# Four plain columns moved ahead of the pairs in down, a 256-column entry for each up quarter, another order of joining, and the ple gate's pairs amid its plain rows

## The chip, the cores and the metric

The kernel runs on one core of a Trainium2 chip. The metric is the device time of one execution in microseconds (us). The kernel before took 1455.88 us, the median of 3 runs (1454.91 to 1456.17). TensorE multiplies matrices, VectorE (DVE in rows, "Vector" here) and ScalarE (ACT) work on tiles, GpSimd (POOL) starts some transfers and SyncE (SP) most of them.

## What is computed

One layer of a decoder trunk on 256 tokens and 2048 channels. The part that the change touches is the channel mixer and the per-layer embedding gate:

```python
u = rmsnorm(h, g_ffn_pre[i])
up = causal_depthwise_conv(u @ w_up[i], conv_w[i], conv_b[i])
gate_ff, value = jnp.split(up, [D_FF], axis=-1)
f = (jax.nn.gelu(gate_ff, approximate=True) * value) @ w_down[i]
h = h + rmsnorm(f, g_ffn_post[i])
e = p[i] @ w_ple_in[i]
h = h + jax.nn.sigmoid((h @ w_ple_gate[i]).astype(jnp.float32)).astype(h.dtype) * e
```

Ahead of it stand two kinds of attention, their gates and an output projection, which are left as they were. D_FF is 5632, so up has 88 columns of 128 channels (gate and value in turn) and down has 44 rows of 128 by 16 columns of 128.

## The kernel before, in words

All numbers are float32. To multiply with enough digits, each operand is split into a high half, which TensorE reads as fp32r, and a low half, the rest. A product is then three matmuls: high by high, low by high, high by low. `three_wide` (L925) does this with 512 columns each. In up (`mul`, L359 on), the activations' two halves lie side by side, 512 columns, so that one 128x128 weight block costs one matmul of 512 columns with the weight's high half (L364) and one of 256 with its low half (L366).

Weights come as tiles of 128x1024, eight blocks, packed in the order of `_plan`. For each tile SP loads `raw` (`load`, L194; 5 buffers), ScalarE writes the high half (`high`, L228) and Vector the low half (`low`, L283; 7 buffers for each half). Whenever TensorE's instruction list comes to a new tile, `tick` runs: it queues deferred work (evacuations of finished banks), the high half of the tile six further on, and the low halves five further on. So the list of each engine interleaves weight preparation with the rest, and the sixth tile ahead can be written only when TensorE has left the tile whose buffer it takes.

The mixer goes in four quarters. In a quarter, up makes 22 columns of 16 blocks each. Each column is summed, scaled, convolved and passed through gelu by ScalarE and Vector in three or four ticks (`up_evac`), which ends in a row of `ft`; there are 11 rows. Then down multiplies the 11 rows by 16 columns:

- the first 8 columns by `strassen` (L1236): rows 0 to 7 make four pairs. A pair takes 21 matmuls of 512 columns where plain ones would be 24, needs sums of weights (two extra tiles a pair, added by Vector at L244 to L248 or by accumulating transfers of POOL into `tsum`, L263), and sums of activations (`mixed`), and collects into seven of the eight banks of 2 KB: P1, P5, P6, P7 and three that go straight to results. After the pairs the rows 8 to 10 follow as plain products ("plains", 36 matmuls) into four result banks. The products are put together by Vector: `join` in quarter 0 (4 operations, L1285 to L1288) or `join_to` later (8, L1294 to L1301), and then `ends` (4, L1305).
- the columns 8 to 11 and 12 to 15 by `four` (L1307), 66 matmuls each into two banks. Their evacuation is two operations, on ScalarE in quarter 0 and on Vector after that (L1394).

In the last quarter the squares of the finished columns (L1344) and their weighing by the gain (`weigh`, L1348) are deferred between these steps; the last two banks are added at L1417, the norm is worked out, applied (L1411) and transposed by TensorE (L1437), while TensorE multiplies the e columns (`e_cols`).

The ple gate (`pg`) does columns 0 to 3 plainly, columns 4 to 11 with `strassen` over 16 rows: rows 8 to 15 plainly, then rows 0 to 7 as four pairs, `join` and `ends` at once, and columns 12 to 15 with `four`. `finish` (L1502 to L1504) multiplies by e, adds h and sends out.

One more detail: where the 512- and 256-column matmuls of up begin after other work, `mm` can do the first eight blocks as three matmuls of 256 columns each (`even=8`, `mul1`, L384 to L386) and turn one later block round (`turned=9`, L363). This pair of settings is called `SETTLE` (L38), and before the change only the column in quarter 0 at which the norm's scale becomes known uses it.

Of the kernel before, what the change touches and what calls it, by code (L numbers as in the profile page):

```python
# [8 lines left out]
F32 = mybir.dt.float32  # L9
F32R = mybir.dt.float32r  # L10
AF = mybir.ActivationFunctionType
OP = mybir.AluOpType
# [35 lines left out]
def _plan():  # L48
# [47 lines left out]
    for q in range(NQ):  # L96
        for n in range(max(FIRST, q * 2 * QT), (q + 1) * 2 * QT):
            add(("up", n), [up[n]], KT)
        rows = list(range(q * QT, (q + 1) * QT))
        down = [("w_down", j) for j in range(KT)]  # L100
        plan.append((("pairs", "down", q), down[:8],
                     paired([(rows[r], rows[r + 1]) for r in range(0, DROWS, 2)]) + whole(rows[DROWS:])))
        for c in (8, 12):
            add(("down", q, c), down[c:c + 4], 0, [[r] for r in rows])
    for c in range(2, 4):
# [4 lines left out]
                 whole(range(2 * PAIRS, KT)) + paired([(2 * p, 2 * p + 1) for p in range(PAIRS)])))  # L110
# [24 lines left out]
def hybrid_block_kernel(ctx: ExitStack, tc: tile.TileContext, head, gx, pT, convp, bias, masks, gains, w, out):  # L135
# [20 lines left out]
    stream, used, sums_of, early_sums = [], 0, {}, []  # L156
    for g in _plan():
        if _pairs(g):
            assert used % 8 == 0
            before = KT - 2 * PAIRS if g[0][:2] == ("pairs", "pg") else 0  # L160
# [16 lines left out]
    half_raw = {sums_of[i] for i in by_dma}  # L177
    place = {r: i for i, r in enumerate(stream) if r is not None}

# [1056 lines left out]
    def strassen(key, src, pairs, plain, first_plain, p1_to):  # L1236
# [11 lines left out]
        def plains(last):  # L1248
            for k in plain:
                w2 = item()  # L1250
                for t in range(2):
                    for n in range(2):
                        add((t, n), cut(src, k, t), w2[n], last and k == plain[-1])

        if first_plain:
            plains(False)
        for p, (k1, k2) in enumerate(pairs):
# [6 lines left out]
            add((0, 1), s[3], w22, last and first_plain)  # L1264
# [7 lines left out]
            add((0, 0), cut(src, k2, 0), w21, last and first_plain)  # L1272
        yield bk
        if not first_plain:
            plains(True)
# [14 lines left out]
    def join_to(o, bk, x):  # L1290

        tt = DVE.tensor_tensor
        x2 = tmp.tile([128, 512], F32, name="x2", tag="s2", bufs=2)
        tt(o[0, 0], o[0, 0], x, OP.add)  # L1294
        tt(x, bk[6], x, OP.add)
        tt(x2, bk[7], x, OP.add)  # L1296
        tt(o[1, 0], o[1, 0], x2, OP.add)
        tt(x, bk[5], x, OP.subtract)
        tt(x2, bk[5], x2, OP.subtract)
        tt(o[0, 1], o[0, 1], x, OP.add)  # L1300
        tt(o[1, 1], o[1, 1], x2, OP.add)  # L1301

    def ends(o, bk):
        for at in ((0, 0), (0, 1), (1, 0), (1, 1)):
            DVE.tensor_tensor(o[at], o[at], bk[at], OP.add)  # L1305

# [47 lines left out]
    for q in range(NQ):  # L1354
        for n in range(max(len(pss), q * 2 * QT), (q + 1) * 2 * QT):
            ps = mm(keys[n], u2, **dict(SETTLE, mid={3: mid}) if n == len(pss) else {})
# [5 lines left out]
        o = quarter(0)  # L1362
        x = o[0, 0] if q == 0 else tmp.tile([128, 512], F32, name="x1", tag="s2", bufs=2)
        s = strassen(("pairs", "down", q), ft, [(r, r + 1) for r in range(0, DROWS, 2)], range(DROWS, QT), False, x)
        bk = next(s)
        defer((None, (lambda bk=bk, o=o: join(o, bk)) if q == 0 else lambda bk=bk, o=o, x=x: join_to(o, bk, x)))
        if end:
            g3 = []
            for n, name in enumerate(("wsum", "tsum")):
                g3.append(fp.tile([128, 1024], F32, name="g3", tag=name))  # L1370
                nc.sync.dma_start(g3[n], gains[:, n * 1024:(n + 1) * 1024])
        next(s)
        defer((None, lambda bk=bk, o=o: ends(o, bk)))
        if end:
            ACT.preload_act_table_set(LNEXP)
            squared(range(2))
        for c in (2, 3):
# [5 lines left out]
            four(("down", q, 4 * c), ps, ft, hold if end and c == 3 else None)  # L1383
            if end and c == 3:
                break
# [9 lines left out]
            defer((lambda evac=evac: evac(False), lambda evac=evac: evac(True)))  # L1395
            if end:
                squared([c])
# [97 lines left out]
    for n in range(PAIRS):  # L1495
        mixture(n)

# [12 lines left out]
    defer((lambda ps=ps: sigmoid(ps, 0), lambda: finish([(t, 0, 512) for t in range(2)])))  # L1510
    o = quarter(512)
    s = strassen(("pairs", "pg"), u3, [(2 * p, 2 * p + 1) for p in range(PAIRS)], range(2 * PAIRS, KT), True, o[0, 0])
    bk = next(s)
    join(o, bk)
    ends(o, bk)
    next(s, None)
# [84 lines left out]
```

## Time and profile before

| | |
|---|---|
| median of 3 runs | 1455.88 us |
| the profiled execution | 1454.63 us |
| its span, first to last instruction | 1452.5 us |
| up, quarter 0, from its settled column on | 642.25 to 731.36 us |
| down, quarters 0 to 3, start | 731.36, 920.37, 1103.82, 1287.64 us |
| down, quarters 0 to 3, end | 796.01, 979.46, 1163.28, 1346.27 us |
| ple gate's last pair's last product to its last matmul | 1418.52 to 1447.53 us |
| mean granted TensorE clock | 0.999 of full speed |

A window's row gives the stretch, its length, the busy time of an engine with its number of instructions, the clock granted to TensorE, the share of the transfer engines' time and GB/s. A row of the timeline gives the start, the length, the engine, the line, the operation with output and input, and in brackets the idle time before it and what ended it. A row of waits gives who waited for whom: the total, how often, the longest.

### The profile page before, as it was taken

To read this page: it belongs to the slowest core of one execution; us is meant where nothing else is said; L and a number is where in the kernel's file an instruction comes from. 1 tells how busy PE (TensorE), PEld (TensorE's weight loads), DVE (VectorE), ACT (ScalarE), POOL (GpSimd) and SP (SyncE) were. 2 spreads that over 40 slices of the span, in tenths; PEclk is the share of its full clock that TensorE was granted. 3 is DMA by queue.
4 is the path that set the end of the run, shared out by engine and by line. 5 is a ranking of instruction groups with operands and counts; after the bars stand their busy time and mean duration, and the time that the engine had idled before them with its cause. 6 is when DMAs were issued, how large, how long until landed. Compare 5 with 4: busy or idle time off the path is not lost.

```text
span 1452.5 us, 20479 instructions
## 1 busy us (share of the span) xinstructions
PE 1433.1 (99%) x7475; PEld 1221.6 (84%) x7475; DVE 1166.5 (80%) x1785; ACT 860.3 (59%) x1295; POOL 39.4 (3%) x49
## 2 busy tenths in 40 slices
PE   9999999999999999999989999999999999999997
PEld 8888888888888888998867888878888788888786
DVE  7876666669889865879996888977889778899696
ACT  7665555566556655676665566645566456566653
POOL 0000000011010000000000000000000000000000
PEclk9999999999999999999999999999999999999999
DMA  7755746479895766464658565586554855558562
GB/s 290 261 176 164 239 151 213 154 235 263 281 248 179 265 238 194 151 237 162 196 176 281 181 190 173 159 284 188 188 180 147 284 187 189 182 138 298 167 219 113
DMA packets 87188, 298.60 MB, mean 206 GB/s; under 512 B 9648, under 2 KB 10288, under 8 KB 86960
## 3 DMA queue, kind: packets, MB, share of 16 engines
q1 hardware_dynamic: 80752, 285.76, 58.4%
q0 software_dynamic: 6336, 11.54, 4.7%
q8 instruction: 59, 0.97, 0.3%
q14 instruction: 41, 0.34, 0.1%
HBM read 294.11 MB, written 3.15 MB: 205 GB/s over the span
## 4 chain that ended last, share of the span: by engine, by line
PE 92%; DVE 3%; DMA 2%; ACT 1%; issue 1%; ACTq 0%; DVEq 0%
PE mm L364 33%; PE mm L927 25%; PE mm L366 17%; PE mm L692 2%; PE mm L690 2%; PE mm L691 2%; PE mm L845 2%; PE mm L847 2%; PE mm L846 2%; DMA raw<-in_w 2%; DVE lo L283 1%; ACT hi L228 1%; DVE lo L275 1%; PE S L364 0%; PE S L703 0%
## 5 line engine op out<-in xcount | busy, mean ns | idle before, releaser
L283 DVE TENSOR_TENSOR lo<-raw,hi 128x1024 fp32r<-128x1024 f32 (+1 forms) x497 | 581.9, 1187 | 115.3 <-ACT hi L228 110.7
L364 PE MATMUL mm<-u,hi 128*128 128x512 f32 x1828 | 643.2, 396 | 0.0
L228 ACT ACTIVATE hi<-raw 128x1024 fp32r<-128x1024 f32 (+1 forms) x497 | 504.5, 1028 | 192.1 <-PE mm L364 61.7
L366 PE MATMUL mm<-u,lo 128*128 128x256 f32 x1818 | 509.9, 281 | 0.0
L364 PEld LDWEIGHTS mm<-u,hi 128*128 128x128 f32 x1828 | 342.3, 188 | 80.1
L366 PEld LDWEIGHTS mm<-u,lo 128*128 128x128 f32 x1818 | 343.4, 189 | 0.8 <-DVE lo L283 0.2
L927 PE MATMUL mm<-hi,ft 128*128 128x512 f32 x544 | 172.4, 391 | 4.1 <-DVE x L1296 2.8
L927 PE MATMUL mm<-hi,u 128*128 128x512 f32 x456 | 147.6, 394 | 3.8 <-DVE ff L1285 3.8
L422 ACT ACTIVATE t<-mm 128x256 f32<-128x256 f32 x131 | 49.8, 380 | 154.3 <-PE mm L366 154.3
L927 PEld LDWEIGHTS mm<-hi,ft 128*128 128x128 f32 x544 | 102.1, 188 | 27.3 <-DVE x L1296 4.0
L927 PE MATMUL mm<-lo,ft 128*128 128x512 f32 x272 | 106.8, 393 | 2.6 <-DVE lo L283 2.6
L927 PEld LDWEIGHTS mm<-hi,u 128*128 128x128 f32 x456 | 86.4, 190 | 22.1 <-DVE ff L1285 4.3
L425 DVE TENSOR_TENSOR s<-mm,t 128x256 f32<-128x256 f32 x116 | 48.9, 422 | 59.7 <-ACT t L422 59.5
L927 PE MATMUL mm<-lo,u 128*128 128x512 f32 x228 | 89.5, 393 | 0.0
L364 PE MATMUL mm<-mg,hi 128*128 128x512 f32 x232 | 80.5, 392 | 0.0
L224 ACT ACTIVATE hi<-wsum 128x512 fp32r<-128x512 f32 x84 | 51.1, 630 | 49.2 <-DVE wsum L247 38.9
L366 PE MATMUL mm<-mg,lo 128*128 128x256 f32 x230 | 64.4, 280 | 0.0
L927 PEld LDWEIGHTS mm<-lo,ft 128*128 128x128 f32 x272 | 51.0, 188 | 15.1 <-DVE lo L283 4.8
L1205 ACT ACTIVATE cv<-cpad,cw 128x256 f32<-128x256 f32 x88 | 52.5, 597 | 10.9 <-DVE cpad L1200 10.7
L275 DVE TENSOR_TENSOR lo<-wsum,hi 128x512 fp32r<-128x512 f32 x84 | 54.3, 685 | 0.3
L927 PE MATMUL mm<-hi,mixed 128*128 128x512 f32 x160 | 52.8, 391 | 0.0
L364 PEld LDWEIGHTS mm<-mg,hi 128*128 128x128 f32 x232 | 43.3, 187 | 9.3
(327 smaller groups left out, 1799.6 us busy)
## 6 DMA issues: line engine op xcount, KB each, us to landing
raw<-in_w SPq DMA_DIRECT2D x479, 512.0 KB, 4.0
gh<-in_w SPq DMA_DIRECT2D x12, 512.0 KB, 5.0
gh<-in_w POOLq DMA_DIRECT2D x24, 256.0 KB, 8.2
raw<-in_w SPq DMA_DIRECT2D x22, 256.0 KB, 3.6
tsum<-in_w SPq DMA_DIRECT2D x10, 512.0 KB, 3.5
tsum<-in_w POOLq DMA_DIRECT2D x20, 256.0 KB, 6.7
hd<-in_head SPq DMA_DIRECT2D x6, 576.0 KB, 7.5
gh<-in_gx SPq DMA_DIRECT2D x6, 512.0 KB, 4.7
```

The source lines that it names most:

```text
L224: ACT.activation(hi[i][:, n * 512:(n + 1) * 512], x, AF.Copy)
L228: ACT.activation(hi[i][:, a:b], raw[i][:, a:b] if src is None else src, AF.Copy)
L275: DVE.tensor_tensor(lo[i][:, to], x, f(hi[i][:, to]), OP.subtract)
L283: DVE.tensor_tensor(lo[i][:, a:b], raw[i][:, a:b] if src is None else src, f(hi[i][:, a:b]), OP.subtract)
L364: PE.matmul(ps, wh, rhs, start=first, stop=last, skip_group_check=True)
L366: PE.matmul(ps[:, :T], wl, rhs[:, :T], start=False, stop=last, skip_group_check=True)
L422: ACT.activation(t1[0], ps[:, T:], AF.Copy)
L425: DVE.tensor_tensor(out, ps[:, :T], t1[0], OP.add)
L690: PE.matmul(pv[t], xh, wh, start=kt == 0, stop=False)
L691: PE.matmul(pv[t], xh, wl, start=False, stop=False)
L927: PE.matmul(ps, x[i], w[j], start=first and n == 0, stop=last and n == 2, skip_group_check=True)
L1205: ACT.activation(y, c[:, 2:], AF.Identity, scale=cw[:, n, 2:3], bias=cw[:, n, 3:4])
```

## The change

Down, in each quarter: columns 8 to 11 are multiplied first, then the pairs, the plains, and columns 12 to 15. Since 44 blocks are five and a half tiles, each of the two groups of four columns is followed by a pad of four blocks that no one reads; the tile with it is loaded and split at half width (`short`). In the last quarter the squares and weighings move accordingly: those of columns 8 to 11 behind the pairs, those of columns 0 to 7 into columns 12 to 15.

Up: the first column of every quarter uses `SETTLE`.

Joining: `join_to` reads the bank of P6 first, then P7, then P5, and the pairs' products of a tile (P6 and a result) change places.

Ple gate: `strassen` takes rows 8 to 13 ahead of the pairs and rows 14 and 15 behind them; `join`, `ends` and the first columns' `finish` are deferred; the sums of activations are deferred behind the first columns' sigmoid.

```diff
+        add(("down", q, 8), down[8:12], 0, [[r] for r in rows])
+        add("pad", down[:4], 0, [rows[:1]])
         plan.append((("pairs", "down", q), down[:8],
                      paired([(rows[r], rows[r + 1]) for r in range(0, DROWS, 2)]) + whole(rows[DROWS:])))
-        for c in (8, 12):
-            add(("down", q, c), down[c:c + 4], 0, [[r] for r in rows])
+        add(("down", q, 12), down[12:], 0, [[r] for r in rows])
+        add("pad", down[:4], 0, [rows[:1]])
...
-                 whole(range(2 * PAIRS, KT)) + paired([(2 * p, 2 * p + 1) for p in range(PAIRS)])))
+                 whole(range(8, 14)) + paired([(2 * p, 2 * p + 1) for p in range(PAIRS)]) + whole(range(14, KT))))
...
-    half_raw = {sums_of[i] for i in by_dma}
     place = {r: i for i, r in enumerate(stream) if r is not None}
+    short = {place[r] for r in short}
+    half_raw = {sums_of[i] for i in by_dma} | short
+    part |= short
...
-    def strassen(key, src, pairs, plain, first_plain, p1_to):
+    def strassen(key, src, pairs, before, after, p1_to):
...
             t2, t4 = item()
+            add((1, 0), cut(src, k2, 1), t4)
             add(6, s[1], t2, last)
-            add((1, 0), cut(src, k2, 1), t4, last and first_plain)
...
+        tt(x2, bk[6], x, OP.add)
         tt(o[0, 0], o[0, 0], x, OP.add)
-        tt(x, bk[6], x, OP.add)
-        tt(x2, bk[7], x, OP.add)
-        tt(o[1, 0], o[1, 0], x2, OP.add)
+        tt(x, bk[7], x2, OP.add)
+        tt(x2, bk[5], x2, OP.subtract)
+        tt(o[1, 0], o[1, 0], x, OP.add)
         tt(x, bk[5], x, OP.subtract)
-        tt(x2, bk[5], x2, OP.subtract)
-        tt(o[0, 1], o[0, 1], x, OP.add)
-        tt(o[1, 1], o[1, 1], x2, OP.add)
+        tt(o[0, 1], o[0, 1], x2, OP.add)
+        tt(o[1, 1], o[1, 1], x, OP.add)
...
-            ps = mm(keys[n], u2, **dict(SETTLE, mid={3: mid}) if n == len(pss) else {})
+            settle = n in (len(pss), q * 2 * QT)
+            ps = mm(keys[n], u2, **SETTLE if settle else {}, mid={3: mid} if n == len(pss) else None)
...
+        plain(2)
         o = quarter(0)
...
+            ACT.preload_act_table_set(LNEXP)
+            squared([2])
         next(s)
         defer((None, lambda bk=bk, o=o: ends(o, bk)))
         if end:
-            ACT.preload_act_table_set(LNEXP)
             squared(range(2))
-        for c in (2, 3):
...
+        ps = plain(3)
...
-    defer((lambda ps=ps: sigmoid(ps, 0), lambda: finish([(t, 0, 512) for t in range(2)])))
+    defer((lambda ps=ps: sigmoid(ps, 0), None))
+    for n in range(PAIRS):
+        mixture(n)
...
     bk = next(s)
-    join(o, bk)
-    ends(o, bk)
-    next(s, None)
+    defer((None, lambda bk=bk, o=o: join(o, bk)))
+    next(s)
+    defer((None, lambda bk=bk, o=o: ends(o, bk)))
+    defer((None, lambda: finish([(t, 0, 512) for t in range(2)])))
```

The order in which the instructions now stand, at three places. The lines of the changed kernel are 6 to 15 higher (L364, L366, L283, L927 are L370, L372, L289, L933). The first place is TensorE in quarter 0, where up ends and down begins. `mm` are banks, `u2` up's activations, `hi` and `lo` weight tiles' halves, `ft` the rows, `mixed` the pairs' sums. Before:

```order
L366 MATMUL mm_7138<-u2_4823,lo_6994 128x256
L927 MATMUL mm_7209<-hi_7023,ft_5995 128x512
L927 MATMUL mm_7209<-lo_7024,ft_5995 128x512
L927 MATMUL mm_7209<-hi_7023,ft_5995 128x512
L927 MATMUL mm_7213<-hi_7023,mixed_6177 128x512
L927 MATMUL mm_7213<-lo_7024,mixed_6177 128x512
```

Now, at the place where the pairs begin, 66 matmuls further on:

```order
L933 MATMUL mm_7188<-lo_7163,ft_5995 128x512
L933 MATMUL mm_7188<-hi_7162,ft_5995 128x512
L933 MATMUL mm_7322<-hi_7191,ft_5995 128x512
L933 MATMUL mm_7322<-lo_7192,ft_5995 128x512
L933 MATMUL mm_7322<-hi_7191,ft_5995 128x512
L933 MATMUL mm_7326<-hi_7191,mixed_6177 128x512
```

The pairs' first tile (`hi_7023` before, `hi_7191` now) stood directly behind up's last block; now it stands behind the four columns' last row.

The second place is TensorE where quarter 1 of up begins, now; `u` are up's activations.

```order
L933 MATMUL mm<-hi,ft 128x512
L390 MATMUL mm<-u_4823,hi 128x256
L391 MATMUL mm<-u_4823,hi 128x256
L392 MATMUL mm<-u_4823,lo 128x256
```

Before, the first block of that column was L364 and L366, 512 and 256 columns, straight after down's last matmul; now eight blocks of three 256-column matmuls come first, then the turned one.

The third place is Vector at the end of down in the last quarter: `lo` and `u3` are low halves of tiles, `ff` the result, `g3` the gain, `sm` small sums of the norm. Before:

```order
L283 TENSOR_TENSOR u3_12431<-raw_12771,u3_12431 128x1024
L283 TENSOR_TENSOR lo_12818<-raw_12789,hi_12817 128x1024
L1394 TENSOR_TENSOR ff_5994<-ff_5994,mm_12713 128x512
L1394 TENSOR_TENSOR ff_5994<-ff_5994,mm_12714 128x512
L283 TENSOR_TENSOR lo_12850<-raw_12809,hi_12849 128x1024
L1348 TENSOR_TENSOR ff_5994<-ff_5994,g3_12646 128x512 x2
L283 TENSOR_TENSOR lo_12874<-raw_12823,hi_12873 128x1024
L1413 TENSOR_REDUCE sm_6178<-sm_6178 128x2
```

Now:

```order
L289 TENSOR_TENSOR u3_12464<-raw_12801,u3_12464 128x1024
L1309 TENSOR_TENSOR ff_5994<-ff_5994,mm_12646 128x512
L1309 TENSOR_TENSOR ff_5994<-ff_5994,mm_12605 128x512
L1309 TENSOR_TENSOR ff_5994<-ff_5994,mm_12630 128x512
L1309 TENSOR_TENSOR ff_5994<-ff_5994,mm_12821 128x512
L289 TENSOR_TENSOR lo_12872<-raw_12833,hi_12871 128x1024
L1357 TENSOR_TENSOR ff_5994<-ff_5994,g3_12792 128x512 x4
L289 TENSOR_TENSOR lo_12908<-raw_12855,hi_12907 128x1024
L289 TENSOR_TENSOR lo_12930<-raw_12877,hi_12929 128x1024
L1427 TENSOR_REDUCE sm_6178<-sm_6178 128x2
```

The evacuation of columns 8 to 11 (L1394) is gone from the end, and the `ends` (L1309, formerly L1305) and the weighing of columns 0 to 7 (four operations, L1357) stand there, which used to lie one group of four columns earlier. Between the join's eighth operation and L1427 there are now a low half, two weighings, a low half, one of half width, and the rows shown.

More of the change, by code (lines that the diff above doesn't have):

```diff
@@ L1246, in add, with plains @@
             three_wide(bk[name], x, w, first, last)
-        def plains(last):
-            for k in plain:
+        def plains(ks):
+            for k in ks:
                 w2 = item()
@@ L1252, in plains @@
                     for n in range(2):
-                        add((t, n), cut(src, k, t), w2[n], last and k == plain[-1])
-        if first_plain:
-            plains(False)
+                        add((t, n), cut(src, k, t), w2[n], k == after[-1])
+        plains(before)
         for p, (k1, k2) in enumerate(pairs):
@@ L1263, in strassen @@
                 ACT.activation(p1_to, bk[1], AF.Copy)
-            add((0, 1), s[3], w22, last and first_plain)
+            add((0, 1), s[3], w22)
             q, t3 = item()
@@ L1268, in strassen @@
             t2, t4 = item()
+            add((1, 0), cut(src, k2, 1), t4)
             add(6, s[1], t2, last)
-            add((1, 0), cut(src, k2, 1), t4, last and first_plain)
             w21, _ = item()
-            add((0, 0), cut(src, k2, 0), w21, last and first_plain)
+            add((0, 0), cut(src, k2, 0), w21)
         yield bk
-        if not first_plain:
-            plains(True)
+        plains(after)
         yield bk
@@ L1305, in ends, with pad @@
             DVE.tensor_tensor(o[at], o[at], bk[at], OP.add)
+    def pad():
+        assert next(plan)[0] == "pad"
+        at["block"] += 4
     def four(key, ps, src, late=None):
@@ L1361, in hybrid_block_kernel, with plain @@
             lend(1, u3)
[L1362 to L1374, printed above, removed]
-            ACT.preload_act_table_set(LNEXP)
-            squared(range(2))
-        for c in (2, 3):
+        def plain(c):
             ps = [bank() for _ in range(2)]
@@ L1382, in hold @@
                 at["hold"] = True
-            four(("down", q, 4 * c), ps, ft, hold if end and c == 3 else None)
-            if end and c == 3:
-                break
+            last = end and c == 3
+            four(("down", q, 4 * c), ps, ft, hold if last else None)
+            pad()
+            if last:
+                return ps
             def evac(low, ps=ps, q=q, c=c):
@@ L1394, in evac @@
                             DVE.tensor_tensor(to, to, ps[t], OP.add)
-            defer((lambda evac=evac: evac(False), lambda evac=evac: evac(True)))
-            if end:
-                squared([c])
+            defer((lambda: evac(False), lambda: evac(True)))
+        plain(2)
+        o = quarter(0)
+        x = o[0, 0] if q == 0 else tmp.tile([128, 512], F32, name="x1", tag="s2", bufs=2)
+        s = strassen(("pairs", "down", q), ft, [(r, r + 1) for r in range(0, DROWS, 2)], [], range(DROWS, QT), x)
+        bk = next(s)
+        defer((None, (lambda bk=bk, o=o: join(o, bk)) if q == 0 else lambda bk=bk, o=o, x=x: join_to(o, bk, x)))
+        if end:
+            g3 = []
+            for n, name in enumerate(("wsum", "tsum")):
+                g3.append(fp.tile([128, 1024], F32, name="g3", tag=name))
+                nc.sync.dma_start(g3[n], gains[:, n * 1024:(n + 1) * 1024])
+            ACT.preload_act_table_set(LNEXP)
+            squared([2])
+        next(s)
+        defer((None, lambda bk=bk, o=o: ends(o, bk)))
+        if end:
+            squared(range(2))
+        ps = plain(3)
     flush()
```

13 lines of the change are left out of this document (8 added, 5 removed).

## The prediction

> **What bounds the kernel now.** I read the page first: its busy times and the chain of work that ended last.
>
> ```profile
> PE 1433.1 (99%) x7475; PEld 1221.6 (84%) x7475; DVE 1166.5 (80%) x1785; ACT 860.3 (59%) x1295; POOL 39.4 (3%) x49
> ...
> PE 92%; DVE 3%; DMA 2%; ACT 1%; issue 1%; ACTq 0%; DVEq 0%
> ```
>
> TensorE carries 92% of the chain, so a change gains only where TensorE stands still or its matmuls follow each other more slowly than they could. The 99% hides that, since a matmul counts as busy for 0.39 us while the next one starts much earlier: the chain, in order of time, has 91 matmuls of 512 columns in 20.63 us, 0.2267 us from start to start. With that price I asked for the windows of the stages that the change touches: down of the four quarters (252 matmuls each, counted with the neighbours at the edges), then the tail of the ple gate (102 of its matmuls).
>
> ```profile
> 1329.89 20.63 PE mm L927 x91
> ```
>
> ```profile
> 731.36:796.01 64.65, 59.74 (x254) 1.00 0.74 233
> 920.37:979.46 59.09, 57.95 (x254) 1.00 0.70 236
> 1103.82:1163.28 59.46, 58.01 (x255) 1.00 0.69 234
> 1287.64:1346.27 58.63, 57.93 (x254) 1.00 0.69 237
> 1418.52:1447.53 29.01, 25.18 (x103) 0.94 0.28 109
> ```
>
> 252 x 0.2267 is 57.1 us. The four downs lose 7.5, 2.0, 2.3 and 1.5 us, 13.3 together; the gate's tail, 23.1 us of work, loses 5.7 (its last matmul runs 0.2 past its successor's place). The waits of TensorE name Vector in all of them:
>
> ```profile
> PE mm L927 <- DVE ff L1285: 3.8, 1, 3.8
> PE mm L927 <- DVE x L1296: 2.8, 3, 1.3
> PE mm L927 <- DVE lo L283: 2.6, 3, 1.4
> PE mm L927 <- DVE ff L1286: 1.3, 1, 1.3
> ```
>
> L283 writes the low halves of weight tiles, which the pairs of quarter 0 wait for; L1285, L1286 and L1296 read a product's bank in the join, and the next four plain columns want that bank. The last view is the up columns:
>
> ```profile
> 642.25:731.36 89.11, 89.11 (x525) 1.00 0.56 183
> 796.01:920.37 124.36, 124.36 (x705) 1.00 0.57 180
> ...
> 1163.28:1287.64 124.36, 124.36 (x706) 1.00 0.58 180
> ```
>
> Quarter 0's last 16 columns take 89.11 us, 5.55 each without the 0.24 of two foreign matmuls; quarters 1 to 3 take 124.36 for 22, 5.65 each, with no wait at all. The same 16 blocks of a 512- and a 256-column matmul come at 0.3467 us each in the one train and 0.3533 in the other. The fast train is the one that began with 256-column matmuls.
>
> **The entry to up.** Its rows in quarter 0:
>
> ```profile
> 642.25 0.28 PE L384 MATMUL mm<-u,hi 128*128 128x256 f32 x1
> ...
> 643.32 0.40 PE L520 MATMUL mm<-sp,ones 128*128 128x256 f32 x2
> 643.56 0.28 PE L384 MATMUL mm<-u,hi 128*128 128x256 f32 x1
> ...
> 645.36 0.40 PE L364 MATMUL mm<-u,hi 128*128 128x512 f32 x1
> ...
> 646.42 0.40 PE L364 MATMUL mm<-u,hi 128*128 128x512 f32 x1
> ```
>
> Eight entry blocks take 3.11 less 0.24, 2.87 us; the three up to the turned one 1.06; the other 341 blocks of a quarter, at 0.3467, 118.2. That is 122.1 against 124.36: 2.2 us a quarter, **6.6 us for three**. If the slow train went on regardless, the entry would cost 0.05 a quarter. I take the fast train, since the trace's only example of this entry led to it. The Trainium skill ("TensorE: Matmul & The Clock Gate", Back-to-back issue gap) lets the spacing depend on the columns alone, N/2.4 + 2.5 ns; by it the entry does nothing, and the sum below would be 6.6 us smaller. The trace does not agree as it stands: equal blocks differ by 6.6 ns.
>
> **Four plain columns ahead of the pairs.** A pair is 21 matmuls, 4.8 us, and eats four tiles of high and low halves, so in the pairs Vector can only live on the lead that it has. In quarter 0 it has little: the sum of the last up column starts 6.9 us after the column's end at 731.36, in quarter 1 only 1.6 us after 920.37.
>
> ```profile
> 738.21 0.42 DVE L425 TENSOR_TENSOR s<-mm,t 128x256 f32<-128x256 f32 x1
> ```
>
> ```profile
> 921.99 0.42 DVE L425 TENSOR_TENSOR s<-mm,t 128x256 f32<-128x256 f32 x1
> ```
>
> The 66 matmuls that now come first last 15.0 us. Vector owes 5.3 us of lag and five and a half low halves, 6.2 us at 1.13 (three of them in 3.4 us, rows below): 11.5. So quarter 0 should enter its pairs with the lead that quarter 1 has today. In quarters 1 to 3 the last column's evacuation, six operations of about 0.42, 2.5 us, leaves the pairs' time and the four columns' own evacuation, two additions of 0.6, comes in. It waits for the last of the 66 matmuls; behind it on Vector (in quarter 0 on ScalarE) stand halves of the next pair, whose buffers come free only then, so nobody waits longer for it. The rows of ft that end late are wanted after 54 matmuls, 12.2 us; the lag of 6.9 and a few operations of 0.4 fit. **The join's order**: the bank that stalls is freed by the join's first operation instead of its third, 1.4 us earlier (1314.71 against 1316.15), and the longest such wait in those quarters was 1.3.
>
> ```profile
> 1314.71 0.69 DVE L1294 TENSOR_TENSOR ff<-ff,x 128x512 f32<-128x512 f32 x1
> ...
> 1316.15 0.69 DVE L1296 TENSOR_TENSOR x<-mm,x 128x512 f32<-128x512 f32 x1
> ...
> 1319.89 3.49 DVE L283 TENSOR_TENSOR lo<-raw,hi 128x1024 fp32r<-128x1024 f32 x3
> 1323.29 2.47 DVE L1305 TENSOR_TENSOR ff<-ff,mm 128x512 f32<-128x512 f32 x4
> ...
> 1326.82 2.49 DVE L1348 TENSOR_TENSOR ff<-ff,g 128x512 f32<-128x512 f32 x4
> ...
> 1333.77 2.51 DVE L283 TENSOR_TENSOR u<-raw,u 128x1024 fp32r<-128x1024 f32 x2
> ...
> 1345.11 0.69 DVE L1417 TENSOR_TENSOR ff<-ff,mm 128x512 f32<-128x512 f32 x1 [1.66 <-PE mm L927]
> 1346.47 0.69 DVE L1417 TENSOR_TENSOR ff<-ff,mm 128x512 f32<-128x512 f32 x1 [0.67 <-PE mm L927]
> ...
> 1349.09 1.28 DVE L1411 SCALAR_TENSOR_TENSOR hx<-ff,sm,hx 128x256 f32<-128x256 f32 x3
> ```
>
> ```profile
> 1350.36 0.60 PE L1437 MATMUL mm<-idf,hx 128*128 128x128 f32 x4
> ```
>
> I leave 0.2, 0.3, 0.5 and 0.2 us of the 13.3: **12.1 gained**, between 10.3 (quarters as they are, quarter 0 like them) and 13.3.
>
> **What comes late instead.** In the last quarter everything that Vector does after the pairs used to lie beside eight plain columns and now lies beside four. The join starts 27.1 us after the pairs (1314.71 less 1287.64); it should again, as Vector is bound there by its own operations and by tile buffers that TensorE frees only as the pairs begin. Behind it stand, by the order shown above: eight join operations 5.2 (1314.71 to 1319.89), six low halves, one of half width, 6.3, two in u 2.5, the ends 2.4, six weighings 3.6, small ones 0.3: 20.3. So Vector is through 47.4 us after the pairs' start, while TensorE ends the last four columns after 27.2 + 15.0 = 42.2. Today Vector waits there for TensorE (1.66 us). The two additions follow and then the norm; the second would start at 48.0, not 42.4: 5.6 late, 0.7 more because ScalarE's squares of both halves then queue, 0.8 less because today's transposes (1350.36) come that long after their input (first of the three at 1349.09). TensorE has only the e columns to do and stands **5.3 us: lost**. Bounds: 3, if the join comes 2.3 sooner, and 8. In quarters 0 to 2 up columns follow, Vector needs only 5.2 + 2.9 + 2.4 before their tiles, and nothing is late.
>
> **Pairs amid the gate.** Today TensorE waits 4.0 us for the join's first operation and then runs at half clock:
>
> ```profile
> 1420.56:1424.56 4.00, 0.17 (x2) 1.00 0.92 349
> 1425.40:1428.80 3.40, 3.40 (x10) 0.50 0.02 10
> ```
>
> Two plain rows, 24 matmuls, 5.4 us, now stand between the pairs and that wait. Against it, Vector does one low half more ahead of the join, and that one waits for its load, which lands 2.2 us after the one before (ScalarE's high halves):
>
> ```profile
> 1421.59 1.06 ACT L228 ACTIVATE hi<-raw 128x1024 fp32r<-128x1024 f32 x1 [1.15 <-DMA raw<-in_w]
> 1423.80 1.06 ACT L228 ACTIVATE hi<-raw 128x1024 fp32r<-128x1024 f32 x1 [1.16 <-DMA raw<-in_w]
> ```
>
> And the pairs come 5.4 us sooner, while Vector is relieved of two low halves (2.3) and of four operations of the first columns' finish (2.6, from 1392.77 to 1395.42), so it is 0.5 later:
>
> ```profile
> 1392.77 0.68 DVE L1502 TENSOR_TENSOR ff<-ff,ee 128x512 f32<-128x512 f32 x1
> ...
> 1395.42 0.69 DVE L275 TENSOR_TENSOR lo<-tsum,hi 128x512 fp32r<-128x512 f32 x1
> ```
>
> Left over: 4.0 + 2.2 + 0.5 - 5.4 = 1.3 us, too short for the half clock, as the waits of 1.3 above were: 5.7 - 1.3, **4.4 gained**, between 2.5 and 5.7. The new pause of 5.3 us at the end of down, however, is longer than the one of 4.0 that halved the clock. The Trainium skill (same page, What's actually happening) puts the gate at an idle window of about 3.4 us, in step with no kernel; the row of 0.50 agrees, 4.0 idle and 3.4 slow. A halved 3.4 us costs at most 1.7; much of what follows waits for Vector anyway, and I take **0.5**.
>
> The short pad tiles add one half-width cast and subtraction each, hidden by ScalarE's idle time and the lead: nothing. SP issues the first two output transfers behind the last weight loads now, with the whole last four columns of the gate still to run, and the gains' two loads a few tiles earlier, past nothing that waits; POOL's queue is unchanged: nothing.
>
> **The sum.** 6.6 + 12.1 + 4.4 - 5.3 - 0.5 = 17.3 us. The profiled execution took 1454.63 us, of which 2.1 lie around the span; that gives 1437.3. The median of the runs is 1455.88, 1.25 higher: **1438.6 us**.
>
> **The rivals.**
> 1. *The last quarter isn't late*: the join starts early enough, and the 5.8 us are not lost. For it: the evacuation leaves the pairs. Against: the high halves' buffers hold Vector back. 1432.8 us, chance 0.13.
> 2. *The entry does nothing*, as the spacing rule has it. For it: no trace shows an entry straight from down. Against: quarter 0. 1438.6 + 6.6 + 0.1 = 1445.3 us, chance 0.12.
> 3. *The pairs stay short of low halves*: the downs keep 2.0, 2.0, 2.3 and 1.5 us, 6.6 more than I leave. For it: pairs ask Vector for about as long as they take. 1445.2 us, chance 0.14.
> 4. *No lead at all, and slower*: Vector comes to the pairs with nothing ready, since the four columns' tiles fill its buffers. It then owes the first five tiles, two full low halves and nine half-width operations of 0.61, 7.8 us, in each quarter, and every such pause halves the clock, 1.5: 4 x 9.3 = 37 us, 1476 us. It decides from 17.3 / 4 = 4.3 us a quarter. Against: 15.0 us for 11.5 of work. Chance 0.04.
>
> That the change doesn't take effect is out: the order above shows it.
>
> **How the numbers follow.** My forecast has 0.55; its own terms span 1433 to 1445. The range 1432 to 1446 takes in rivals 1 to 3. A measurement can tell about 0.2% here, 2.9 us; all cases but the fourth lie well below 1453. Faster 0.94, the same 0.02, slower 0.04.
>
> **What would show it.** Up windows of 122 us in quarters 1 to 3; down windows under 58 us; a pause of about 5 us before the first transposes after down, with Vector busy through it; about 1 us at the gate's last four columns and no row of clock 0.50 there. I am wrong if up keeps 124.4, if waits for low halves stay in the pairs, or if no pause follows down.

## The result, and the profile after

| | before | after |
|---|---|---|
| median (runs) | 1455.39 us (4) | 1441.39 us (4) |
| lowest to highest | 1452.49 to 1456.17 | 1440.70 to 1443.66 |
| the profiled execution, its span | 1454.63, 1452.5 us | 1441.72, 1439.7 us |

The change makes the kernel 14.0 us faster: the ratio is 0.991, with a 95% interval of 0.9892 to 0.9928. The forecast was 1438.6 us with a range of 1432 to 1446, so the result lies inside it, 2.8 us above the number. The terms did not all come out, and that is what the experiments are about. The sum itself was further off than the number: it gives 1437.3 us for the profiled execution, which took 1441.72, 4.4 us more. The other 1.6 us are scatter of the runs: the profiled run before lay 1.25 us below the median that the forecast started from, and the one after lies 0.3 above its own.

The page after, busy times and the shares of the chain that ended last:

```profile
PE 1425.5 (99%) x7499; PEld 1222.9 (85%) x7499; DVE 1167.3 (81%) x1789; ACT 860.0 (60%) x1299; POOL 39.4 (3%) x49
...
PE 93%; DVE 4%; ACT 1%; issue 1%; DMA 1%; ACTq 0%; DVEq 0%
```

TensorE still carries the chain; its share went up by one point. What each stage gained is read from windows of TensorE, one for each stage from the settled column of quarter 0 on: stretch, its length, busy time, clock, DMA share, GB/s. The rows left out are up of quarters 2 and 3, 122.15 each, and down of quarter 2, 57.98. After:

```profile
642.33:731.89 89.56, 89.56 (x526) 1.00 0.59 188
731.89:789.05 57.16, 57.16 (x254) 1.00 0.77 239
789.05:911.21 122.16, 122.16 (x714) 1.00 0.60 193
911.21:969.19 57.98, 57.75 (x255) 1.00 0.64 206
...
1271.47:1329.45 57.98, 57.75 (x254) 1.00 0.64 207
1329.45:1362.39 32.94, 27.69 (x130) 0.95 0.58 180
1362.39:1434.49 72.10, 70.10 (x303) 1.00 0.54 175
```

And before, the last two stretches, which the prediction did not show whole (from the end of down to the last transposes, and from there to the last matmul):

```profile
1346.27:1373.53 27.26, 25.90 (x130) 1.00 0.51 158
1373.53:1447.53 74.00, 70.17 (x303) 0.98 0.52 171
```

| stage | forecast of the gain | by the windows |
|---|---|---|
| up, quarters 1 to 3 | 6.6 | 124.36 - 122.15, three times: 6.6 |
| down, four quarters | 12.1 | 7.5 + 1.1 + 1.5 + 0.7 = 10.7 |
| end of down to the last transposes | -5.8 | 27.26 - 32.94 = -5.7 |
| from there to the last matmul (most of the gate) | 4.4 | 74.00 - 72.10 = 1.9 |
| sum | 17.3 | 13.5 |

The difference of the two spans, 12.8 us, is this sum less 0.5 us ahead of down in quarter 0 and 0.2 behind the last matmul. The first row after begins 0.45 us ahead of the settled column, whose first matmul stands at 642.78; from there to down are 89.11 us, as before. So the 0.5 us lie ahead of that column, and they are scatter: over the kernels below, which are nearly the same up to there, down in quarter 0 begins anywhere from 731.1 to 733.3 us.

All waits of TensorE from quarter 0's down to the end, after: who waited for whom, total, times, longest.

```profile
PE mm L1451 <- DVE hx L1425: 5.2, 4, 3.1
PE mm L933 <- DVE ff L1289: 0.9, 1, 0.9
PE mm L933 <- DVE lo L281: 0.4, 2, 0.2
PE mm L933 <- ACT hi L230: 0.4, 1, 0.4
```

L1451 are the transposes behind down, which wait for the applied norm; L1289 is the gate's join, 0.9 where 3.8 stood; the last two rows are new, halves of weight sums in the gate's pairs. The waits for low halves in quarter 0 of down and for the join's banks are gone.

The end of down, Vector first, after. The rows give start, length, line, operation and, in brackets, idle time and what ended it:

```profile
1327.46 1.21 DVE L289 TENSOR_TENSOR lo<-raw,hi 128x1024 fp32r<-128x1024 f32 x1
1328.60 2.49 DVE L1357 TENSOR_TENSOR ff<-ff,g 128x512 f32<-128x512 f32 x4
1331.01 2.35 DVE L289 TENSOR_TENSOR lo<-raw,hi 128x1024 fp32r<-128x1024 f32 x2
...
1333.54 1.28 DVE L1431 TENSOR_TENSOR ff<-ff,mm 128x512 f32<-128x512 f32 x2
```

Down ends at 1329.45 (its window above), and Vector comes to the last two banks only at 1333.54, behind a low half, four weighings and two low halves. What TensorE does then, and the clock granted to it:

```profile
1329.45 4.24 PE L933 MATMUL mm<-u,pTs 128*128 128x512 f32 x18
1336.75 0.33 PE L1451 MATMUL mm<-idf,hx 128*128 128x128 f32 x1 [3.06 <-DVE hx L1425]
1337.93 0.90 PE L1451 MATMUL mm<-idf,hx 128*128 128x128 f32 x3 [0.85 <-DVE hx L1425]
1338.48 2.74 PE L933 MATMUL mm<-u,pTs 128*128 128x512 f32 x6
```

```profile
1337.50:1340.50 3.00, 2.57 (x8) 0.50 0.69 269
```

From start to start and less the work itself, the two pauses ahead of the first transposes are 3.2 and 1.1 us, 4.3 together (the other two waits for the norm, 1.3 in all, stood in the profile before with 1.4); the other 1.4 of the 5.7 us is the half clock. The forecast had 5.3 and 0.5.

The gate's pairs, TensorE, after:

```profile
1397.50 0.50 PE L933 MATMUL mm<-hi,u 128*128 128x512 f32 x1 [0.41 <-ACT hi L230]
1398.23 0.50 PE L933 MATMUL mm<-lo,u 128*128 128x512 f32 x1 [0.22 <-DVE lo L281]
...
1413.12 0.50 PE L933 MATMUL mm<-hi,u 128*128 128x512 f32 x1 [0.91 <-DVE ff L1289]
```

The join costs 1.2 us from start to start, where 1.3 was forecast. The other rows are single pauses of a few tenths, each followed by a matmul that is 0.11 us longer; with those too short for brackets, TensorE loses 2.6 us in the pairs, nearly all of it between 1393.6 and 1404.3, where the gate before lost nothing (68.3 us of work and the tail's 5.7 are its 74.00). With the join's 1.2 these 2.6 us make the 3.8 that the gate still loses of 5.7; the term lacks 2.5.

### The profile page after: what moved, and what is told of

It reads as the page before. It is cut to its first block, busy times and chain, and to the rows that moved or that the text cites. A ratio compares the mean times of both kernels' runs of the same rounds, so it can differ in the third digit from the quotient of the medians.

```text
span 1439.7 us, 20545 instructions
## 1 busy us (share of the span) xinstructions
PE 1425.5 (99%) x7499; PEld 1222.9 (85%) x7499; DVE 1167.3 (81%) x1789; ACT 860.0 (60%) x1299; POOL 39.4 (3%) x49
## 4 chain that ended last, share of the span: by engine, by line
PE 93%; DVE 4%; ACT 1%; issue 1%; DMA 1%; ACTq 0%; DVEq 0%
PE mm L370 32%; PE mm L933 26%; PE mm L372 17%; PE mm L698 2%; PE mm L696 2%; PE mm L697 2%; PE mm L853 2%; PE mm L852 2%; PE mm L851 2%; DVE lo L289 1%; DVE lo L281 1%; DMA raw<-in_w 1%; ACT hi L234 1%; PE S L370 0%; PE mm L392 0%
## 5 line engine op out<-in xcount | busy, mean ns | idle before, releaser
L289 DVE TENSOR_TENSOR lo<-raw,hi 128x1024 fp32r<-128x1024 f32 (+1 forms) x501 | 582.2, 1178 | 99.1 <-ACT hi L234 94.2
L370 PE MATMUL mm<-u,hi 128*128 128x512 f32 x1804 | 628.1, 392 | 0.0
L372 PE MATMUL mm<-u,lo 128*128 128x256 f32 x1791 | 501.4, 280 | 0.0
L370 PEld LDWEIGHTS mm<-u,hi 128*128 128x128 f32 x1804 | 336.7, 187 | 73.0
L372 PEld LDWEIGHTS mm<-u,lo 128*128 128x128 f32 x1791 | 338.4, 189 | 0.7
L933 PE MATMUL mm<-hi,ft 128*128 128x512 f32 x544 | 173.4, 389 | 0.0
L933 PE MATMUL mm<-hi,u 128*128 128x512 f32 x456 | 147.3, 392 | 1.3 <-DVE ff L1289 0.9
L933 PEld LDWEIGHTS mm<-hi,ft 128*128 128x128 f32 x544 | 102.1, 188 | 21.1
L933 PE MATMUL mm<-lo,ft 128*128 128x512 f32 x272 | 106.2, 390 | 0.4
L933 PEld LDWEIGHTS mm<-hi,u 128*128 128x128 f32 x456 | 85.6, 188 | 19.6 <-DVE ff L1289 1.3
L933 PE MATMUL mm<-lo,u 128*128 128x512 f32 x228 | 89.1, 391 | 0.5 <-DVE lo L281 0.2
L370 PE MATMUL mm<-mg,hi 128*128 128x512 f32 x232 | 80.5, 392 | 0.0
L372 PE MATMUL mm<-mg,lo 128*128 128x256 f32 x230 | 64.4, 280 | 0.0
L933 PEld LDWEIGHTS mm<-lo,ft 128*128 128x128 f32 x272 | 51.0, 188 | 12.2 <-DVE lo L281 1.7
L281 DVE TENSOR_TENSOR lo<-wsum,hi 128x512 fp32r<-128x512 f32 x84 | 54.4, 685 | 7.3 <-ACT hi L230 7.0
L1211 ACT ACTIVATE cv<-cpad,cw 128x256 f32<-128x256 f32 x88 | 52.5, 596 | 12.1 <-DVE cpad L1206 12.0
L933 PE MATMUL mm<-hi,mixed 128*128 128x512 f32 x160 | 55.9, 390 | 0.0
L933 PEld LDWEIGHTS mm<-lo,u 128*128 128x128 f32 x228 | 42.8, 188 | 10.2 <-DVE lo L281 1.1
```

What stands on the lines that cost most here:

```text
L281: DVE.tensor_tensor(lo[i][:, to], x, f(hi[i][:, to]), OP.subtract)
L289: DVE.tensor_tensor(lo[i][:, a:b], raw[i][:, a:b] if src is None else src, f(hi[i][:, a:b]), OP.subtract)
L370: PE.matmul(ps, wh, rhs, start=first, stop=last, skip_group_check=True)
L372: PE.matmul(ps[:, :T], wl, rhs[:, :T], start=False, stop=last, skip_group_check=True)
L933: PE.matmul(ps, x[i], w[j], start=first and n == 0, stop=last and n == 2, skip_group_check=True)
L1211: ACT.activation(y, c[:, 2:], AF.Identity, scale=cw[:, n, 2:3], bias=cw[:, n, 3:4])
```

## The experiments

Every kernel here computes all of the reference. Times are medians; the kernel before took 1455.0 to 1455.4 us on the same chips.

### The entry alone

The kernel before with these lines in up:

```diff
-            ps = mm(keys[n], u2, **dict(SETTLE, mid={3: mid}) if n == len(pss) else {})
+            settle = n in (len(pss), q * 2 * QT)
+            ps = mm(keys[n], u2, **SETTLE if settle else {}, mid={3: mid} if n == len(pss) else None)
```

> The kernel before with nothing but the 256-column entry in quarters 1 to 3. Theory (the entry sets the train): the three up windows go from 124.36 to 122.1 us, 2.2 us each, the time falls by 6.6 us to about 1448.8; downs, the end of down and the gate stay as they were. Rival (the spacing depends on the columns alone): 124.4 us each and 1455.4 us.

Measured: 1448.73 us (1447.2 to 1449.7), ratio 0.9953 (0.9938 to 0.9967): 6.7 us faster. Quarter 1's window of up, the others are equal to it:

```profile
795.31:917.46 122.15, 122.15 (x713) 1.00 0.58 184
```

The entry is worth its 6.6 us without anything else. A spacing that depends on the columns alone is refuted: 352 blocks take 124.36 or 122.15 us, and of these 341 are the same, a 512- and a 256-column matmul.

### Which part of the entry does it

Two kernels, each the one after with half of the entry in quarters 1 to 3. The first:

```diff
-            ps = mm(keys[n], u2, **SETTLE if settle else {}, mid={3: mid} if n == len(pss) else None)
+            ps = mm(keys[n], u2, **(SETTLE if n == len(pss) else dict(even=8)) if settle else {}, mid={3: mid} if n == len(pss) else None)
```

The second has `dict(turned=9)` in that place.

> The kernel after, but the entry of quarters 1 to 3 has only its eight blocks of 256-column matmuls, and no block with the low half first. Theory (a run of 256-column matmuls sets the fast train): the up windows stay at 122.1 us, 1441.4 us. Rival (the block with the low half first sets it): 124.4 us, 2.2 us more in each of three quarters, 1448.0 us.

> The kernel after, but the entry of quarters 1 to 3 has only the one block with the low half first (the tenth), and no run of 256-column matmuls. Theory now (that block, which puts two 256-column matmuls and then two of 512 next to each other, sets the fast train alone): nine blocks at 0.3533 and the rest at 0.3467, 122.1 us a window, 1441.4 us. Rival (both parts together are needed): 124.4 us, 1448.0 us.

Measured: 1450.31 and 1450.21 us, one run each. Quarter 1's windows, `even` alone and then `turned` alone:

```profile
790.46:914.88 124.42, 124.42 (x713) 1.00 0.59 191
```

```profile
789.37:913.74 124.37, 124.37 (x706) 1.00 0.60 191
```

Both theories fell, one after the other: neither the run of 256-column matmuls nor the block with the low half first leads to the fast train. It takes both, eight even blocks and then a turned one behind a normal one. Why, no run shows. The times are some 2 us above the 1448.0 us of the rival; the up windows don't show them, and with one run each they are left open.

### The last quarter in the order of before

The kernel after, with `OLD_Q = 3`:

```diff
-        add(("down", q, 8), down[8:12], 0, [[r] for r in rows])
-        add("pad", down[:4], 0, [rows[:1]])
+        old = q == OLD_Q
+        if not old:
+            add(("down", q, 8), down[8:12], 0, [[r] for r in rows])
+            add("pad", down[:4], 0, [rows[:1]])
         plan.append((("pairs", "down", q), down[:8],
...
+        if old:
+            add(("down", q, 8), down[8:12], 0, [[r] for r in rows])
         add(("down", q, 12), down[12:], 0, [[r] for r in rows])
-        add("pad", down[:4], 0, [rows[:1]])
+        if not old:
+            add("pad", down[:4], 0, [rows[:1]])
...
-        plain(2)
+        if q != OLD_Q:
+            plain(2)
...
+        if q == OLD_Q:
+            plain(2)
+            if end:
+                squared([2])
         ps = plain(3)
```

> The kernel after, but the last quarter of down in the order of before: pairs first, then eight plain columns, no short tiles there. Theory (Vector has only four columns beside it after the pairs, and is late): the stretch from the end of down to the start of the gate, 32.9 us after and 27.3 before, is 27.3 again, the last down loses 1.5 us as before and not 0.85, so 5.0 us less than the kernel after: about 1436.4 us. Rival (the pause comes from the loads or from ScalarE's squares, not from the order): 32.9 us stay, and the time is 1441.4 or 0.7 us more.

Measured: 1436.29 us (1434.58 to 1438.74), ratio 0.9868 (0.9852 to 0.9884), 5.1 us less than after. Down in quarter 3, and the stretch behind it:

```profile
1271.97:1330.18 58.21, 57.86 (x255) 1.00 0.71 241
1330.18:1357.44 27.26, 25.91 (x129) 1.00 0.54 152
```

The order of the last quarter costs the 5.7 us, and gives only 0.2 for them: with the pairs first, that quarter loses 1.1 us beside its 57.1 of work and not 0.85.

### Quarter 0 in the order of before

The same edit with `OLD_Q = 0`.

> The kernel after, but quarter 0 of down in the order of before. Theory (the four columns give Vector its lead): its down window goes from 57.2 back to 64.6 us, all else stays, 7.5 us more than after: about 1448.9 us. Rival (the loss of quarter 0 went because of other edits, the order in which products are multiplied among them): 57 to 60 us, 1441 to 1444 us.

Measured: 1448.16 us (1447.0 to 1449.51), ratio 0.995 (0.9935 to 0.9965), 6.8 us more than after. Down in quarter 0, and what TensorE mostly waits for there:

```profile
731.17:794.83 63.66, 60.77 (x254) 0.97 0.75 235
```

```profile
PE mm L939 <- DVE lo L295: 1.7, 2, 1.4
PE mm L939 <- DVE lo L287: 0.8, 1, 0.8
```

The waits for low halves are back (L295 and L287 are the low halves of tiles and of sums here). Of quarter 0's 7.5 us, 6.5 come from the four columns ahead of the pairs. The last 1.0 lies in edits that this kernel keeps; it wasn't taken apart.

### The join's order

The kernel after, with the eight operations of `join_to` as they were:

```diff
-        tt(x2, bk[6], x, OP.add)
         tt(o[0, 0], o[0, 0], x, OP.add)
-        tt(x, bk[7], x2, OP.add)
-        tt(x2, bk[5], x2, OP.subtract)
-        tt(o[1, 0], o[1, 0], x, OP.add)
+        tt(x, bk[6], x, OP.add)
+        tt(x2, bk[7], x, OP.add)
+        tt(o[1, 0], o[1, 0], x2, OP.add)
         tt(x, bk[5], x, OP.subtract)
-        tt(o[0, 1], o[0, 1], x2, OP.add)
-        tt(o[1, 1], o[1, 1], x, OP.add)
+        tt(x2, bk[5], x2, OP.subtract)
+        tt(o[0, 1], o[0, 1], x, OP.add)
+        tt(o[1, 1], o[1, 1], x2, OP.add)
```

> The kernel after, with the eight operations of the join in quarters 1 to 3 in the order of before. Theory of now (the join's first operation begins 2.1 us before the four columns want the bank, so its order no longer decides): the downs stay at 58.0 us, 1441.4 us. Rival (the prediction's term: freeing the bank 1.4 us earlier is what saves the wait of up to 1.3 us): up to 1.3 us more in each of three quarters, 59.3 us, 1445.3 us.

Measured: 1443.09 us, one run. Down in quarters 1 and 2:

```profile
911.05:969.65 58.60, 58.05 (x254) 1.00 0.67 207
1091.81:1150.63 58.82, 58.05 (x255) 1.00 0.66 206
```

Neither expectation came out: 0.6 and 0.8 us more in quarters 1 and 2, 1.5 together, nothing in quarter 3. The margin of 2.1 us that I counted on was quarter 3's. In quarter 1 the join comes later. Vector in the kernel after, then TensorE with the old order:

```profile
953.52 0.68 DVE L1298 TENSOR_TENSOR x<-mm,x 128x512 f32<-128x512 f32 x1
```

```profile
955.24 0.50 PE L933 MATMUL mm<-hi,ft 128*128 128x512 f32 x1 [0.32 <-DVE x L1299]
```

TensorE wants the bank at about 954.8 us. The first operation of the join is through at 954.2; with the old order it is the second that frees the bank, and that one ends at 955.2. So the order is worth something only where the join's margin is under one operation of 0.7 us. The 1.3 us for each quarter was an upper end.

### Weighings behind the last additions

The kernel after, with the four weighings of columns 0 to 7 put off:

```diff
...
-            squared(range(2))
+            squared(range(2), True)
...
         DVE.tensor_tensor(to, to, ps[t], OP.add)
+        weigh(t, 0)
         square_to(t, 3)
...
+    for t in range(2):
+        weigh(t, 1)
     keep_e(0)
```

> The kernel after, but in the last quarter the four weighings of the paired columns come behind the last two additions of down, two beside ScalarE's squares and two behind the first transposes. Theory (Vector's queue ahead of those additions makes the pause): the additions start 2.4 us sooner, the pause of 3.1 + 0.9 us shrinks to about 2 and no half clock follows (1.4 us), so the stretch is 29 to 30 us instead of 32.9: 1438.0 us, between 1437.4 and 1439.0. Rival (the pause waits for ScalarE, or for loads): 32.9 us and 1441.4 us. If the half clock stays for some other reason than the pause's length: 30.8 us, 1439.3 us.

Measured: 1440.59 us (1439.49 to 1441.75), ratio 0.9898 (0.9883 to 0.9913). The stretch, and the clock in it:

```profile
1330.12:1361.83 31.71, 27.94 (x129) 0.95 0.60 182
1337.50:1340.50 3.00, 3.00 (x10) 0.50 0.49 201
```

Only 1.2 us of the stretch went, and the half clock stayed. Vector shows why:

```profile
1327.45 1.22 DVE L289 TENSOR_TENSOR lo<-raw,hi 128x1024 fp32r<-128x1024 f32 x1
1329.96 2.36 DVE L289 TENSOR_TENSOR lo<-raw,hi 128x1024 fp32r<-128x1024 f32 x2 [1.29 <-ACT hi L234]
...
1332.50 0.68 DVE L1432 TENSOR_TENSOR ff<-ff,mm 128x512 f32<-128x512 f32 x1
```

Where the weighings had stood, Vector now waits 1.29 us for a high half, which itself waits for its load. The additions start 2.4 us behind down's end, where they started 4.1 behind it; they were to start 1.7. Taking work out of a queue ahead of a wait turns part of it into idle time.

### Low halves behind them, too

The kernel of the last experiment, with a cap on the low halves from the last four columns on:

```diff
...
-            lows(max(before, min(i + 2, at["high"])))
+            lows(min(at["cap"], max(before, min(i + 2, at["high"]))))
...
             def hold():
-                lows(at["high"])
                 at["hold"] = True
...
+        if end:
+            at["cap"] = lent[-1] + 1
         ps = plain(3)
...
         apply(0, 256, [t])
+    at["cap"] = NI
+    lows(lent[-1] + 2)
```

> The kernel after, with the weighings late as in the experiment before, and besides the three low halves for the gate's first columns, which Vector made ahead of the last two additions of down, behind them. Theory (Vector's queue makes the pause: low halves and their wait for a load stood where the weighings had been): the additions start with TensorE's last matmul of down, 3.6 us sooner than after, no pause before the first transposes, no half clock, the stretch is 27.3 to 28.3 us instead of 32.9, 1436 to 1437 us. Rival (the norm's chain of squares and small operations sets the pause): about 31 us, 1439.5 us or more.

Measured: 1438.09 us (1437.77 to 1438.64), ratio 0.9882 (0.9865 to 0.9898), 3.3 us less than after. Vector's first of the two additions, then the stretch on TensorE:

```profile
1328.92 0.68 DVE L1433 TENSOR_TENSOR ff<-ff,mm 128x512 f32<-128x512 f32 x1
```

```profile
1329.48:1357.89 28.41, 26.74 (x129) 1.00 0.64 204
```

The addition starts 0.6 us ahead of the end of down, the pause before the first transposes and the half clock are gone, and 4.5 of the 5.7 us come back in the stretch. It is 1.2 longer than with the old order, since the gate's first matmuls now wait for Vector, which does there what was put off (0.8 us for a low half of the activations, 0.4 for one of a tile, by the waits). So the pause was Vector's queue, low halves and weighings together, and not the norm's own chain. The stretch is just above the 28.3 us expected, and the time fell 1.2 us less than the stretch. That is only half told: the gate's own window was 0.5 us longer in this trace, since TensorE waited 1.4 us and not 0.9 for the join; the rest is within the scatter of the runs.

### Seven rows ahead of the gate's pairs

The kernel after, with `range(8, 15), range(15, KT)` for the plain rows ahead of and behind the pairs, instead of `range(8, 14), range(14, KT)`, and with the place of the weight sums in the stream moved along by one tile.

> The kernel after, but seven plain rows of the gate ahead of its pairs and one behind them, instead of six and two. After: TensorE loses 2.7 us inside the pairs to low halves and 1.2 us to the join. Theory (Vector is full from the pairs' first halves to the join, so rows only choose where TensorE waits for it): about 1.3 in the pairs and 2.5 at the join, 3.5 to 4.2 in all as before this edit, 1441.4 us within 0.5. Rival (the prediction's: the pairs have what they need, only the rows behind them cover the join): 2.7 us in the pairs stay and the join costs 3.9 us, 1444.1 us.

Measured: 1444.53 us, one run. The gate's window (after: 72.10), and the longest wait in it:

```profile
1361.95:1437.13 75.18, 70.87 (x303) 0.98 0.51 168
```

```profile
PE mm L933 <- DVE ff L1289: 4.0, 1, 4.0
```

The time is the rival's (1444.1), but not by its parts. The pairs lose 1.0 us instead of 2.6: one more row ahead does give them 1.6, against the rival. The join costs 4.2, and a half clock behind it 1.6 more. So the loss is not merely moved either, as the theory had it: pairs and join together lose 5.2 us where they lost 3.8, and the long wait at the join brings the half clock with it.

### The mixtures made earlier

The kernel after, with the four mixtures queued during the gate's first four columns:

```diff
         if k % 2 and k < KT - 2:
             ahead()
+        if k in (4, 6, 8, 10):
+            mixture((k - 4) // 2)
...
-    for n in range(PAIRS):
-        mixture(n)
```

> The kernel after, but the four mixtures of the gate's activations (six operations of Vector and ScalarE each, on Vector 1.7 us each, 6.7 in all) are made during the gate's first four columns, where Vector stands idle for 9 of 24 us, instead of behind them. Theory (in the gate's pairs TensorE waits because Vector's work is full): of the 2.7 us in the pairs and the 1.2 us at the join at least 3 go, 1438.2 us, between 1437.5 and 1438.8. Rival (the low halves there wait for loads or for ScalarE): both stay, 1441.4 us. If the first four columns then wait for Vector themselves: 1440 us or more, with the loss before the gate's pairs.

Measured: 1437.31 us (1434.67 to 1437.75), ratio 0.9872 (0.9856 to 0.9889), 4.1 us less than after, just under the range expected. The gate on TensorE:

```profile
1362.36:1430.68 68.32, 68.32 (x303) 1.00 0.59 192
```

No wait is left in it, neither in the pairs nor at the join: 3.8 us of the window. Vector's busy time up to the pairs' first sums and from there to about the pairs' end, in the kernel after, and then in this one:

```profile
1362.39:1384.96 22.57, 18.94 (x35) 1.00 0.59 194
1384.96:1405.23 20.27, 19.88 (x30) 1.00 0.65 174
```

```profile
1362.36:1384.96 22.60, 20.54 (x29) 1.00 0.74 240
1384.96:1402.64 17.68, 17.32 (x25) 1.00 0.69 193
```

In both kernels Vector is 98% busy in the pairs. What differs is how far it is ahead when they begin. The last of the sums of activations shows it, in the kernel before and in the kernel after:

```profile
1392.17 0.68 DVE L1191 TENSOR_TENSOR mixed<-y,mixed 128x512 fp32r<-128x512 f32 x1
```

```profile
1386.71 0.68 DVE L1197 TENSOR_TENSOR mixed<-y,mixed 128x512 fp32r<-128x512 f32 x1
```

Before, it ended 8.7 us ahead of the pairs' first matmul (1401.52); after, 2.4 us behind it (1384.96). ScalarE's part of the mixtures moved with them, so this run alone doesn't tell the two engines apart; but in these pairs ScalarE itself waits 3.3 us for weight sums that Vector makes (L253), so the queue that is full is Vector's.

### Versions that beat both

Two kernels: the last quarter in the order of before with the early mixtures; and the late weighings and low halves with the early mixtures.

> The kernel after, with the last quarter of down in the order of before and the gate's mixtures made during its first four columns: 5.1 and 4.1 us less, since they lie in different stages: 1432.2 us, between 1431.2 and 1433.4. Rival (the two share Vector's time behind down): 1434 us or more.

> The kernel after, with weighings and low halves behind the last two additions of down and the gate's mixtures made during its first four columns: if both do what each should alone, 4.4 to 5.6 and 4.1 us less, 1431.7 to 1432.9 us. Rival (what was put off now meets the mixtures in Vector's idle 9 us): 1434 us or more, with waits in the gate's first four columns.

Measured: 1432.70 us (1431.91 to 1433.30), ratio 0.9843 (0.9829 to 0.9858), and 1432.49 us (1432.33 to 1433.89), ratio 0.9844 (0.983 to 0.9859). The stretch behind down and the gate, in the first of the two:

```profile
1328.97:1356.22 27.25, 25.89 (x129) 1.00 0.45 136
1356.22:1424.55 68.33, 68.33 (x303) 1.00 0.58 192
```

By the windows the savings add up, as they lie in different stages: 5.7 + 3.8 us in the first, 4.7 + 3.8 in the second (28.26 and 68.31 us). By the medians the first gains 8.7 us, where 5.1 and 4.1 were gained alone, and the second 8.9, where 3.3 and 4.1 were. The two versions can't be told apart; both are 22 to 23 us faster than the kernel before and 9 faster than the one after.

## Why the prediction was right, and where not

**The entry** was right in mechanism and size: 6.6 us forecast, 6.6 in the windows, 6.7 alone. The rival that it does nothing fell with 122.15 against 124.36 us. For it speaks the Trainium skill ("TensorE: Matmul & The Clock Gate", Back-to-back issue gap), whose formula for the gap goes by the columns alone. The section gives that formula for an isolated matmul, though, and says that in a stream with weight loads both operations set the spacing. By the formula a block would take 0.325 us, an estimate from that page; the traces have 0.3467 and 0.3533. But the reason given, that the fast train "began with 256-column matmuls", is not enough: with those alone it stays slow.

**Four columns ahead of the pairs** was right in quarter 0: 57.16 us, where 57.3 was forecast, and undoing it brings the waits for low halves back. The term was 1.4 us too big. "I leave 0.2, 0.3, 0.5 and 0.2 us" was too little for quarters 1 to 3, which keep 0.85 each, in short pauses inside the pairs; the trace shows them before low-half matmuls, each 0.2 to 0.3 with 0.11 behind it, and the weight loads there wait for the low halves of weight sums (L281). Of the join's order, "1.3" was the longest of three waits (2.8 us in all before); in the kernel after it is worth 1.5 us.

**What comes late in the last quarter** came out in size, 5.8 forecast and 5.7 measured, and the place and the cause were as told: Vector is through 47.1 us after the pairs' start (1333.54 less 1286.43, 66 matmuls behind 1271.47), where 47.4 was forecast. That the size fits is in part luck, since errors cancelled. The join began 25.9 us after the pairs' start (at 1312.33) and not 27.1, and what stands behind it took 21.2 us and not 20.3, 1.1 of them a wait for a high half. TensorE ended the last four columns after 43.0 us and not 42.2, for the short pauses inside the pairs. So the pauses were 4.3 us instead of 5.3 (the terms as written, 5.6 + 0.7 - 0.8, even make 5.5), and the half clock cost 1.4 instead of 0.5. "Much of what follows waits for Vector anyway" was the wrong step: in all but 0.5 of the 3.4 us at half clock TensorE had work ready.

**Pairs amid the gate** is the step that failed, 1.9 us instead of 4.4. TensorE waited 1.2 us at the join where 1.3 was forecast, but this is luck: it came to the join 2.6 us late, so the join came some 2.5 us later than the sum has it. What was left out is the other end: "the pairs come 5.4 us sooner" was booked as time for the join alone, but it is also 5.4 us less for Vector ahead of the pairs, while the mixtures stood in that very stretch. The same sum of lead that the prediction made for down (Vector's debt against the plain matmuls ahead) was not made for the gate. The experiment with the early mixtures shows that it was this: with four mixtures of 1.7 us each moved to where Vector stood idle, both losses go.

Rival 1, the last quarter not late, was wrong for the change; the old order there, or low halves and weighings put off, show what it is worth to avoid the lateness, 5.1 and 3.3 us. Rival 3 was half right: halves are late in the pairs, in quarters 1 to 3 of down for 0.85 us each and in the gate for 2.6. Rival 4 did not occur.

## What to carry to other kernels

Plain work ahead of a stage that eats prepared tiles faster than they are made gives that stage a lead; count the lead at every place where the order changes, at both ends of the stage moved. An order that helps in three repetitions can cost in the last one, where the work behind it is of another kind: there the old order can stay. Before a wait is shortened by taking work out of a queue, look at what in that queue waits for a load.

## What the runs showed that was not expected

The train of a 512- and a 256-column matmul has two stable spacings, 0.3467 and 0.3533 us a block; eight blocks of 256-column matmuls and a turned block together lead to the fast one, each by itself to the slow one.

TensorE's clock fell to half without one long pause. In the kernel with the late weighings it stood for 1.9 and 1.0 us, with one transpose between; the clock was 0.50 from about 1337.4 to 1340.8 us. The Trainium skill ("TensorE: Matmul & The Clock Gate", What's actually happening) describes a free-running window of about 3.4 us that has to be idle. The 3.4 us at half clock agree with its length, but the whole of it need not be idle: here the pauses made 2.9 us in all, with a transpose between. With the early mixtures the clock fell at 1335.8 us, when TensorE had stood for 2.2 us, and came back at 1342.6, after twice 3.4 us. With seven rows ahead of the gate's pairs it fell at 1415.5 us, and of the 3.4 us before that TensorE had stood for 2.1. Pauses of 1.2 and 0.6 us, as at 1344 us in the kernel after, did nothing.

After each short wait of TensorE for a weight half, the next matmul took 0.11 us longer from start to start (0.34 instead of 0.2267), so that a wait costs that on top.
